# A two-layer hybrid encoder trunk on one core: mixers and norms emitted in fine parts between runs of dense matmuls

## The chip, the cores and the metric

The kernel runs on one core of a Trainium2 chip. The metric is the device time of one execution in microseconds. Three runs of the kernel before took 2494.32, 2494.62 and 2501.36 us; the median is 2494.62 us.

## The reference, cut to what matters

The input x is 1024 tokens of 1024 features, float32. Two layers are applied, each with its own weights:

```python
h = x
for l in range(2):
    mixed = hybrid_mixer(rmsnorm(h, norm_pre_mix[l]), ...)          # w_in -> 3 mixers -> w_out
    h = h + rmsnorm(mixed, norm_post_mix[l])
    ff = squared_relu_mlp(rmsnorm(h, norm_pre_ffn[l]), w_ff1[l], w_ff2[l])   # 1024 -> 4096 -> 1024
    h = h + rmsnorm(ff, norm_post_ffn[l])
return h
```

`hybrid_mixer` projects its normalised input once. From the columns it feeds three causal token mixers: an mLSTM (4 heads of 128 values), a gated linear attention (4 heads of 64) and a retention (4 heads of 64). All carry a state along the sequence. Each head's output is normalised and gated, and the concatenation goes through `w_out`. `rmsnorm` needs the sum of squares of a token over all 1024 features before any feature of it can go on.

## The kernel before, in words

**Tiling.** The sequence is cut into two halves of 512 tokens. A layer and a half make a unit with four dense stages: the input projection (`main`, 8 column groups, then `gates`, 4 groups), the output projection `out_proj` (4 groups), and the MLP `ffn_steps` (8 chunks of 512 hidden features; each chunk has two `f1` groups and four `f2` groups, so 16 and 32 steps). Dense work stands in `fm_group` and `tm_group`. Every float32 product is made of three float32r matmuls (`mm3`, L217 to L220). A group of `fm_group` with 1024 rows holds 48 matmuls of 512 columns, one with 512 rows (`f2`) holds 24; a group of `tm_group` holds 96 matmuls of 256 to 272 columns.

**Weights.** `wslot` (L206) brings 512 rows of a weight: a DMA into `raw`, a copy on ScalarE into `whi`, a subtraction on VectorE into `wlo`. Each of the three has 3 buffers, and all loads are requested 6000 places ahead in the order of the groups.

**Mixers.** `mixer` (L397) does 256 tokens, so each unit has two passes. A pass has gate rows (a transpose `rt`, scans, a second transpose `st`), a convolution, the GLA scores in seven levels (operands `Qg`, `Kg` on VectorE, then the matmuls `gs`), the rotary step, and for each of two chunks of 128 tokens: mLSTM scores `ms`, numerator `mn`, state `mk` and `mu`, retention scores `rs`, outputs `gr`, states `gk` and `gu`, the head norms on ScalarE and VectorE, and transposes `yp` with a product `gt` (L702) that is stored to `pj.y` in DRAM (L703). `load_y` (L718) reads it back, one tile of 128 features for all 512 tokens at a time, and splits it for `out_proj`; so each tile that `out_proj` reads needs the last chunk of the unit.

**Norms.** `post_norm` and `pre_norm` take a sum of squares `ss`, spread it over the partitions with a float32 matmul by ones (`nps_...`, L277), make 1/sqrt on ScalarE and VectorE, and then go through 8 tiles. `mix_norms` runs after `out_proj` (post_mix, sum of squares, pre_ffn), `ffn_norms` after the MLP (post_ffn, sum of squares, the next layer's pre_mix or the output).

**Order.** The kernel is written as one stream of instructions. A scheduler at build time makes each engine's fixed order from it: of the instructions that it takes to be ready, the one with the earliest place in the stream goes first. `tc.high_priority(offset=n)` moves a place n instructions ahead: 6000 for weights, 9000 for emptying PSUM, 2500 for norms. At run time the orders do not change, and an engine whose next instruction is not ready waits.

In the stream, the mixer of layer 0, half 0 stands whole between its unit's `gates` and the next unit's `main` (L997). The three other mixers are spread over the MLP of the other half by `weave` (L825): six parts at the first step, then 1.3 parts a step, of 56 parts. `mix_norms` and `ffn_norms` stand in one piece, 2500 places ahead.

Of the kernel before, what the change touches and what calls it, by code (L numbers as in the profile page):

```python
# [46 lines left out]
def hybrid_trunk(ctx, tc, a, out):  # L47
# [50 lines left out]
    # ---------------------------------------------------------------- parameters  # L98
    # rows of 128 features, transposed on the tensor engine
# [44 lines left out]
    def rotary(hold):  # L144
# [32 lines left out]
        # every later function is in this one set  # L177
# [13 lines left out]
    # block-diagonal operands and states, zero off the blocks  # L191
# [30 lines left out]
    def split(src, name):  # L222
        """float32 [P, 512] as two float32r parts that sum to it."""
# [6 lines left out]
    def fm_group(w, u, evac, name):  # L230
        """w: [1024 or 512, 256] weight columns; out: features on partitions, 2 tiles."""
# [3 lines left out]
        for k in range(nk):  # L235
            for m in range(2):
# [4 lines left out]
                if k == nk - 1:  # L241
                    with tc.high_priority(offset=EPRIO):
                        rest = evac(m, ps[m])
                    if rest:
                        with tc.high_priority(offset=RPRIO):
                            rest()

    def tm_group(w, u, evac, name):
        """w: [1024, n] weight columns; out: tokens on partitions, one tile a chunk."""
        n = w.shape[1]  # L250
        sl = [wslot(w[512 * k:512 * (k + 1), :], n, f"{name}_{k}") for k in range(2)]
        for c in range(NC):
# [15 lines left out]
    def newton(r, v, t):  # L268
        """One step of r <- 1/sqrt(v); v and t are lost."""
# [4 lines left out]
    def rstd_of(ss, name):  # L274
        """1/sqrt(mean over features + eps) on every partition, from the sums of squares."""
        ps = psc.tile([P, 512], F32, tag="sc", name=f"nps_{name}")
        PE.matmul(ps, ones, ss, start=True, stop=True)  # L277
        v = np_.tile([P, TH], F32, tag="nt", name=f"nv_{name}", bufs=3)
# [19 lines left out]
    def pre_norm(h, l, key, name):  # L298
        """h: 8 tiles of the residual; returns the normalised input, split."""
        r = rstd_of(square_sum(h, name), name)  # L300
# [7 lines left out]
    def post_norm(half, acc, ss, l, key, name, store):  # L308
        """acc: 8 tiles of a block's output, turned in place into the new residual."""
        r = rstd_of(ss, name)  # L310
# [9 lines left out]
    # ---------------------------------------------------------------- input projection  # L320
# [12 lines left out]
    def gate_evac(pj, t0, silu):  # L333
        """norm gain * sigmoid (or silu) of a projection, to DRAM."""
# [19 lines left out]
    def in_groups(pj, u):  # L354
        """The column groups of the input projection, as closures."""
# [41 lines left out]
    def mixer(pj, prev, q):  # L397
        """Tokens q*256 ... of a half (q is 0 or 1): all three mixers, to pj.y; yields between its parts."""
# [10 lines left out]
        # gate rows  # L409
# [32 lines left out]
        S.activation(out=st[32:36, :], in_=m[:, 1:], func=AF.Exp, scale=-1.0)  # L442
        ps = ptr.tile([P, 512], F32, tag="tr", name=f"st{nm}")
# [6 lines left out]
        # causal depthwise convolution and silu of the mLSTM's q and k  # L450
# [29 lines left out]
        # GLA: decays and the scores of two chunks  # L480
# [32 lines left out]
        ready = level_operands(0, LEVELS[0])  # L513
        # scores on the diagonal
        qk = m1.tile([P, QT], F32, tag="ge", name=f"qk{nm}", bufs=2)
        V.tensor_tensor(out=qk, in0=gq, in1=gk, op=ALU.mult)
        ps = psc.tile([P, 512], F32, tag="sc", name=f"dd{nm}")
        for c in range(2):
            mm = PE.matmul(ps[:, 4 * c:4 * c + 4], qk[:, c * P:(c + 1) * P], hsel, start=True, stop=True)
            if c == 0:  # L520
                behind(mm, ready)
# [4 lines left out]
        G.tensor_tensor(out=Pg8, in0=ident.unsqueeze(1).to_broadcast([P, 8, P]), in1=dd.unsqueeze(2).to_broadcast([P, 8, P]), op=ALU.mult)  # L526
        for li, s in enumerate(LEVELS):
# [24 lines left out]
        # retention: rotary  # L552
# [13 lines left out]
        for c in range(2):  # L566
# [41 lines left out]
            # state  # L608
# [4 lines left out]
            V.tensor_tensor(out=kw, in0=ps[:, 0:256].rearrange("p (h d) -> p h d", h=4), in1=wk.unsqueeze(2).to_broadcast([P, 4, 64]), op=ALU.mult)  # L613
            for r in range(2):
                ps = ptr.tile([P, 512], F32, tag="tr", name=f"mu{cn}_{r}")
# [7 lines left out]
            # ---- retention scores  # L623
            for h in range(4):
                hs = slice(32 * h, 32 * h + 32)
                S.copy(out=Qr[hs, h, :], in_=rqk[hs, 0, cs])
# [8 lines left out]
            # ---- GLA and retention outputs  # L635
# [5 lines left out]
            for h in range(4):  # L641
# [3 lines left out]
            # ---- GLA and retention states  # L645
# [6 lines left out]
                            in1=gout[:, 0:4].unsqueeze(2).to_broadcast([P, 4, 32]), op=ALU.mult)  # L652
            ps = ptr.tile([P, 512], F32, tag="tr", name=f"gu{cn}")
# [10 lines left out]
            # ---- head norms  # L664
# [79 lines left out]
    def block_sq(ss, src, sq, kt):  # L744
        """ss += src^2; sq: scratch."""
# [341 lines left out]
```

## Time and profile before

| | |
|---|---|
| median of three runs | 2494.62 us (2494.32 to 2501.36) |
| span of the profiled execution | 2496.7 us, from the first to the last instruction |
| what lies around the span | the profiled execution's own time is not listed apart from the three runs; its span is 2.1 us above their median |
| TensorE busy | 2425.6 us |
| VectorE, ScalarE, GpSimd busy | 1554.9, 1064.5, 255.8 us |
| DMA, mean over the span | 129 GB/s |

The busy time of a matmul in the profile overlaps that of the next one, since they are pipelined: a dense matmul of 512 columns is shown with about 400 ns, while the next one starts some 231 ns later. So starts are to be compared, and waits; the busy share alone says little. Names such as `d_f` stand for the PSUM tile of a group (`d_in`, `d_out`, `d_f` for input projection, output projection, MLP), and numbers of buffers are left out of names.

### The profile page before, as it was taken

The page shows a single profiled execution, that of the slowest core. Times are in us where ns is not written, and L with a number is a line of the kernel's source. Part 1 is how long each engine was busy: PE and PEld are TensorE (multiplying, and loading weights), DVE is VectorE, ACT ScalarE, POOL GpSimd, SP SyncE. Part 2 cuts the span into 40 slices and gives each one's busy share as a digit, 9 for nine tenths or more (in the row PEclk, how much of TensorE's full clock was granted, in tenths as well). Part 3 has the DMA queues.
Part 4 walks back from the last instruction along what each step waited for, and adds up shares of the span by engine and source line. Part 5 has one row for each costly group of instructions (what it writes and reads, how often), then busy time and mean ns, then how long its engine had stood idle before and what let it go on. Part 6 is the DMA issues. An engine that isn't in the chain of part 4 may idle for free.

```text
span 2496.7 us, 31320 instructions
## 1 busy us (share of the span) xinstructions
PE 2425.6 (97%) x11436; PEld 1978.3 (79%) x11436; DVE 1554.9 (62%) x2882; ACT 1064.5 (43%) x2035; POOL 255.8 (10%) x249
## 2 busy tenths in 40 slices
PE   7999999999999999999999999999999999999998
PEld 7887787787788788788788778878878877788886
DVE  5659958847655775665855487475685448634344
ACT  5664457334332554633423255563333345332223
POOL 2100000101101110011100111011010101111110
PEclk9999999999999999999999999999999999999999
DMA  7754455334232565433323355633332344433231
GB/s 232 221 144 144 137 173 185 91 110 123 77 107 90 163 205 178 133 99 102 116 87 102 106 178 181 182 121 95 117 109 83 90 134 152 143 93 93 93 99 62
DMA packets 323670, 321.61 MB, mean 129 GB/s; under 512 B 15370, under 2 KB 292412, under 8 KB 323516
## 3 DMA queue, kind: packets, MB, share of 16 engines
q1 hardware_dynamic: 323516, 319.61, 41.6%
q8 instruction: 90, 1.47, 0.3%
q14 instruction: 64, 0.52, 0.1%
HBM read 263.92 MB, written 55.64 MB: 128 GB/s over the span
## 4 chain that ended last, share of the span: by engine, by line
PE 55%; issue 18%; DVE 13%; DMA 3%; POOL 3%; ACT 2%; SPq 0%; POOLq 0%; DVEq 0%; ACTq 0%
PE d_f L218 10%; PE d_f L219 10%; PE d_f L220 10%; PE d_in L219 4%; PE d_in L218 4%; PE d_in L220 4%; POOL r_hid L769 3%; PE d_out L219 2%; PE d_out L218 2%; PE d_out L220 2%; DVE Qg L510 1%; DMA hl_pm<-hD 1%; DVE l_f L214 1%; PE gs L533 1%; DVE Pg L537 1%
## 5 line engine op out<-in xcount | busy, mean ns | idle before, releaser
L213 ACT CAST h_f<-r_f 128x1024 fp32r<-128x1024 f32 x256 | 267.8, 1046 | 662.5 <-PE d_f L220 656.8
L214 DVE TENSOR_TENSOR l_f<-r_f,h_f 128x1024 fp32r<-128x1024 f32 x256 | 321.2, 1255 | 204.2 <-ACT h_f L213 203.3
L218 PE MATMUL d_f<-h_hid,l_f 128*128 128x512 f32 x1024 | 413.4, 404 | 2.1 <-DVE f L789 2.1
L218 PE MATMUL d_f<-uh_uf,l_f 128*128 128x512 f32 x1024 | 409.4, 400 | 1.6 <-ACT uh_uf L226 1.6
L219 PE MATMUL d_f<-l_hid,h_f 128*128 128x512 f32 x1024 | 407.1, 398 | 2.1 <-DVE l_hid L770 2.1
L219 PE MATMUL d_f<-ul_uf,h_f 128*128 128x512 f32 x1024 | 408.2, 399 | 0.6 <-DVE ul_uf L227 0.5
L220 PE MATMUL d_f<-h_hid,h_f 128*128 128x512 f32 x1024 | 405.4, 396 | 0.0
L220 PE MATMUL d_f<-uh_uf,h_f 128*128 128x512 f32 x1024 | 405.1, 396 | 0.0
L769 POOL TENSOR_TENSOR r_hid<-r_hid 128x512 f32<-128x512 f32 x128 | 165.2, 1290 | 1140.7 <-ACT h_hid L768 1112.2
L789 DVE TENSOR_TENSOR f<-f,d_f 128x512 f32<-128x512 f32 x224 | 153.3, 684 | 155.6 <-PE d_f L220 154.4
L218 PEld LDWEIGHTS d_f<-h_hid,l_f 128*128 128x128 f32 x1024 | 193.0, 189 | 49.7 <-DVE f L789 5.0
L218 PEld LDWEIGHTS d_f<-uh_uf,l_f 128*128 128x128 f32 x1024 | 192.7, 188 | 47.6 <-issue 2.3
L219 PEld LDWEIGHTS d_f<-l_hid,h_f 128*128 128x128 f32 x1024 | 192.6, 188 | 44.6 <-DVE l_hid L770 3.4
L220 PEld LDWEIGHTS d_f<-uh_uf,h_f 128*128 128x128 f32 x1024 | 192.4, 188 | 44.7 <-issue 0.9
L219 PEld LDWEIGHTS d_f<-ul_uf,h_f 128*128 128x128 f32 x1024 | 192.5, 188 | 43.9 <-DVE ul_uf L227 1.8
L220 PEld LDWEIGHTS d_f<-h_hid,h_f 128*128 128x128 f32 x1024 | 192.4, 188 | 43.7 <-issue 0.2
L770 DVE TENSOR_TENSOR l_hid<-r_hid,h_hid 128x512 fp32r<-128x512 f32 x128 | 88.3, 690 | 181.7 <-POOL r_hid L769 181.7
L214 DVE TENSOR_TENSOR l_in<-r_in,h_in 128x1024 fp32r<-128x1024 f32 (+2 forms) x96 | 118.8, 1238 | 74.0 <-ACT h_in L213 72.1
L765 ACT ACTIVATE r_hid<-d_f 128x512 f32<-128x512 f32 x128 | 76.5, 598 | 182.4 <-PE d_f L220 182.4
L213 ACT CAST h_in<-r_in 128x1024 fp32r<-128x1024 f32 (+2 forms) x96 | 101.3, 1055 | 43.2 <-PE d_in L220 29.0
L218 PE MATMUL d_in<-uh_x,l_in 128*128 128x512 f32 x256 | 104.7, 409 | 2.3 <-ACT pv L369 1.8
L219 PE MATMUL d_in<-ul_x,h_in 128*128 128x512 f32 x256 | 103.6, 405 | 0.0
(356 smaller groups left out, 4214.5 us busy)
## 6 DMA issues: line engine op xcount, KB each, us to landing
r_f<-in_w_ff_dram SPq DMA_DIRECT2D x256, 512.0 KB, 3.6
r_in<-in_w_in_dram SPq DMA_DIRECT2D x80, 512.0 KB, 3.9
r_out<-in_w_out_dram SPq DMA_DIRECT2D x32, 512.0 KB, 3.5
pv<-pv SPq DMA_DIRECT2D x64, 128.0 KB, 2.7
hl_pm<-hD SPq DMA_DIRECT2D x32, 256.0 KB, 4.4
pf<-px SPq DMA_DIRECT2D x32, 256.0 KB, 4.3
vt<-pv SPq DMA_DIRECT2D x32, 256.0 KB, 3.8
pg<-gz_g SPq DMA_DIRECT2D x32, 256.0 KB, 2.3
```

The costliest lines, as they stand in the source:

```text
L213: S.copy(out=hi[:, :, :n], in_=raw[:, :, :n])
L214: V.tensor_tensor(out=lo[:, :, :n], in0=raw[:, :, :n], in1=hi[:, :, :n].bitcast(F32), op=ALU.subtract)
L218: PE.matmul(ps, al, bh, start=start, stop=False)
L219: PE.matmul(ps, ah, bl, start=False, stop=False)
L220: PE.matmul(ps, ah, bh, start=False, stop=stop)
L510: V.tensor_tensor(out=qb[hs, h, :].rearrange("p (n s) -> p n s", s=s), in0=gqv[hs, :, 1, :], in1=ev[hs, :, 1, :], op=ALU.mult)
L533: mm = PE.matmul(ps[:, c * 256:(c + 1) * 256], kb[:, c * P:(c + 1) * P], qb[:, :, c * 64:(c + 1) * 64], start=True, stop=True)
L537: V.copy_predicated(out=Pg.rearrange("p c h (n w s) -> p (c h) n w s", w=2, s=s)[:, :, :, 1, :], mask=lvm[:, li * 64:(li + 1) * 64].rearra ...
L765: S.activation(out=r, in_=ps, func=AF.Relu)
L769: G.tensor_tensor(out=r, in0=r, in1=r, op=ALU.mult)
L770: V.tensor_tensor(out=lo, in0=r, in1=hi.bitcast(F32), op=ALU.subtract)
L789: V.tensor_tensor(out=t, in0=t, in1=ps, op=ALU.add)
```

## The change

`side`, `tick`, `beside` and `flush` are new. A generator is put beside the dense work with a rate; each call of `tick` adds the rate to its account and advances it by one part for each whole unit. `fm_group` calls `tick` after every 12 matmuls, `tm_group` after every 24 of its half as wide ones. `weave` goes. The mixer has 37 parts in a pass instead of 28: the producers on ScalarE and VectorE of some matmuls stand one part ahead of them. The second `mu` matmul uses another PSUM pool. The two `behind` edges of the diagonal scores go. `mix_norms` and `ffn_norms` become generators: they start after two ticks and let seven ticks pass between the two norms, and the matmul by ones stands at its place in the stream, no longer 2500 places ahead. Removed comments are not shown.

```diff
+    side = []
+    def tick():
+        for g in list(side):
+            g[2] += g[1]
+            while g[2] >= 1 and g in side:
+                g[2] -= 1
+                if next(g[0], 0) == 0:
+                    side.remove(g)
+    def beside(gen, rate=1.0, due=0.0):
+        g = [gen, rate, due]
+        side.append(g)
+        return g
+    def flush(*gs):
+        for g in gs:
+            if g in side:
+                side.remove(g)
+                for _ in g[0]:
+                    pass
...
 # fm_group, for each k and m; tm_group, for each chunk
+                tick()
...
     def rstd_of(ss, name):
+        return rstd_end(rstd_begin(ss, name), ss, name)
+    def rstd_begin(ss, name):
         ps = psc.tile([P, 512], F32, tag="sc", name=f"nps_{name}")
         PE.matmul(ps, ones, ss, start=True, stop=True)
+        return ps
...
 # mixer: new yields after the gate rows' last activation, after qk and the first
 # level's operands, after Pg, after the Qm copies, after kw (with the Qr copies,
 # which stood after the state), and after kt_
             for r in range(2):
-                ps = ptr.tile([P, 512], F32, tag="tr", name=f"mu{cn}_{r}")
+                ps = (psc if r else ptr).tile([P, 512], F32, tag="sc" if r else "tr", name=f"mu{cn}_{r}")
...
-    def weave(parts, steps):
...
-    def mix_norms(l, half, acc, ss):
+    def mix_norms(l, half, acc, ss, res, gap):
+        for _ in range(gap[0]):
+            yield 1
+        n = f"pm{l}{half}"
+        ps = rstd_begin(ss, n)
         with tc.high_priority(offset=NPRIO):
-            h = post_norm(half, acc, ss, l, "post_mix", f"pm{l}{half}", True)
-            return pre_norm(h, l, "pre_ffn", f"uf{l}{half}"), h
+            h = post_norm_end(half, acc, rstd_end(ps, ss, n), l, "post_mix", n, True)
+            n = f"uf{l}{half}"
+            ss = square_sum(h, n)
+        for _ in range(gap[1]):
+            yield 1
+        ps = rstd_begin(ss, n)
+        with tc.high_priority(offset=NPRIO):
+            res["u"] = pre_norm_end(h, rstd_end(ps, ss, n), l, "pre_ffn", n)
+        res["h"] = h
... # ffn_norms in the same way; final yields after each of its 4 chunks
+    AFTER, NEXT = 2, 7
+    MIX = 0.58
-    run(main[2:] + gates)
-    for _ in mix(pj[0, 0], None):
-        pass
+    run(main[2:])
+    m = beside(mix(pj[0, 0], None), 1.35)
+    run(gates)
     pj[0, 1] = Proj(0, 1)
     main, gates = in_groups(pj[0, 1], u[1])
     run(main)
+    flush(m)
     o = out_proj(pj[0, 0], load_y(pj[0, 0]))
-    uf0, _ = mix_norms(0, 0, *o)
+    r = {}
+    g = beside(mix_norms(0, 0, *o, r, (AFTER, NEXT)))
     run(gates)
-    steps, st = ffn_steps(0, 0, uf0)
-    weave(mix(pj[0, 1], pj[0, 0]), steps)
+    flush(g)
+    steps, st = ffn_steps(0, 0, r["u"])
+    m = beside(mix(pj[0, 1], pj[0, 0]), MIX)
+    run(steps)
+    flush(m)
     y = load_y(pj[0, 1])
-    u[0] = ffn_norms(0, 0, st)
+    g = beside(ffn_norms(0, 0, st, r, (AFTER, NEXT)))
     o = out_proj(pj[0, 1], y, mixer_tiles("01"))
-    uf1, _ = mix_norms(0, 1, *o)
+    flush(g)
     pj[1, 0] = Proj(1, 0)
-    main, gates = in_groups(pj[1, 0], u[0])
-    run(main + gates)
-    steps, st = ffn_steps(0, 1, uf1)
-    weave(mix(pj[1, 0], None), steps)
+    main, gates = in_groups(pj[1, 0], r["u"])
+    g = beside(mix_norms(0, 1, *o, r, (AFTER, NEXT)))
+    run(main)
+    flush(g)
+    m = beside(mix(pj[1, 0], None), MIX)
+    run(gates)
+    steps, st = ffn_steps(0, 1, r["u"])
+    run(steps)
+    flush(m)
... # layer 1 likewise; its last mixer is beside gates and steps[:-7]:
+    run(steps[:-7])
+    flush(m)
     o = out_proj(pj[1, 1], load_y(pj[1, 1]), mixer_tiles("11"))
+    g = beside(mix_norms(1, 1, *o, r, (AFTER, NEXT)))
     run(steps[-7:])
+    flush(g)
+    done, finish = last_norm(1, residual_tokens(r["h"]))
+    g = beside(ffn_norms(1, 0, st, r, (AFTER, 2)), 0.5)
     steps, st = ffn_steps(1, 1, r["u"], done=done)
     run(steps)
+    flush(g)
```

## Rows read from the trace of the kernel before

**Rows 1.** The profile's page: busy us of each engine, share of span, instructions.

```profile
PE 2425.6 (97%) x11436; PEld 1978.3 (79%) x11436; DVE 1554.9 (62%) x2882; ACT 1064.5 (43%) x2035; POOL 255.8 (10%) x249
```

**Rows 2.** Waits of TensorE, whole span: waiter, awaited, total us, times, longest.

```profile
PE gs L533 <- DVE Kg L511: 10.0, 11, 1.7
PE nps_uf L277 <- DVE ss_uf L295: 8.2, 4, 2.5
PE nps_u L277 <- DVE ss_u L295: 4.0, 2, 2.2
PE mn L602 <- DVE qi L597: 3.9, 2, 2.1
PE mu L616 <- DVE Cst L620: 3.1, 4, 0.9
...
PE ops L920 <- DVE f L315: 2.4, 4, 0.8
PE d_f L218 <- DVE f L789: 2.1, 4, 0.5
...
PE st L445 <- ACT gi L439: 1.9, 2, 1.3
```

**Rows 3.** Windows by stage: us, then busy of each engine, clock, DMA share, GB/s.

```profile
127.90:172.40 44.50, 43.23 (x180) 34.98 (x181) 18.55 (x22) 30.55 (x47) 0.00 (x0) 0.96 0.52 147
172.40:327.60 155.20, 147.82 (x886) 126.17 (x885) 140.48 (x399) 74.32 (x222) 5.30 (x9) 1.00 0.50 151
...
423.20:846.50 423.30, 412.84 (x1845) 331.06 (x1844) 272.54 (x532) 157.35 (x323) 47.89 (x45) 1.00 0.35 105
846.50:894.80 48.30, 46.45 (x197) 36.64 (x197) 40.83 (x52) 28.51 (x44) 8.97 (x4) 1.00 0.56 176
894.80:1034.60 139.80, 137.88 (x774) 119.51 (x773) 82.75 (x122) 75.98 (x118) 6.67 (x5) 1.00 0.59 181
...
2067.80:2112.00 44.20, 42.28 (x181) 32.79 (x180) 40.17 (x53) 22.56 (x33) 7.14 (x4) 1.00 0.56 179
2112.00:2496.70 384.70, 371.49 (x1645) 298.18 (x1643) 177.52 (x216) 125.22 (x171) 41.90 (x32) 0.99 0.31 96
```

**Rows 4.** Timeline, layer 0 half 0, mixer's last chunk to out_proj: start us, us, engine.

```profile
291.55 1.03 PE L587 MATMUL ms<-Qm,mqk 128*128 128x256 f32 x4
...
315.78 0.68 DVE L702 TENSOR_TENSOR gt<-yp,gt 128x512 f32<-128x512 f32 x1
...
327.65 0.39 PE L218 MATMUL d_out<-uh_y,l_out 128*128 128x512 f32 x1
...
371.89 0.39 PE L220 MATMUL d_out<-uh_y,h_out 128*128 128x512 f32 x1
```

**Rows 5.** Tiles py, ul_y and gt: duration ns min/median/max; DMA landing us (py, ul_y).

```profile
DMA to landing us min/median/max: 2.3/3.8/4.7
...
DMA to landing us min/median/max: 3.2/3.8/4.7
...
L725 ACT CAST uh_y<-ul_y x32: 603/618/626, 321.3 to 2030.7; 128x512 fp32r<-128x512 f32 x32
L702 DVE TENSOR_TENSOR gt<-yp,gt x32: 681/686/692, 225.3 to 2008.4; 128x512 f32<-128x512 f32 x32
```

**Rows 6.** Timeline of SP's queue: weights of out_proj are issued from here.

```profile
820.17 0.37 SPq L210 DMA_DIRECT2D r_out<-in_w_out_dram  x1
```

**Rows 7.** Timeline of TensorE: the two matmuls by ones of mix_norms(0, 0).

```profile
375.83 1.07 PE L277 MATMUL nps_pm<-sso,ones 128*128 128x512 f32 x2
...
409.51 1.88 PE L277 MATMUL nps_uf<-ss_uf,ones 128*128 128x512 f32 x2 [2.38 <-DVE ss_uf L295]
```

**Rows 8.** Timeline of VectorE: last tiles of two pre-norms.

```profile
434.33 1.27 DVE L227 TENSOR_TENSOR ul_uf<-w_uf,uh_uf 128x512 fp32r<-128x512 f32 x2
...
898.02 0.68 DVE L227 TENSOR_TENSOR ul_u<-w_u,uh_u 128x512 fp32r<-128x512 f32 x1
```

**Rows 9.** Window after the wait in rows 7, columns as in rows 3.

```profile
409.50:413.50 4.00, 3.99 (x9) 2.50 (x10) 2.74 (x4) 4.00 (x8) 0.00 (x0) 0.57 0.71 240
```

More of the change, by code (lines that the diff above doesn't have):

```diff
@@ L260, in tm_group @@
                 evac(c, ps)
+            tick()
     def sumsq_add(ss, sq, first, eng=V):
@@ L298, in pre_norm, with pre_norm_end @@
     def pre_norm(h, l, key, name):
-        r = rstd_of(square_sum(h, name), name)
+        ss = square_sum(h, name)
+        return pre_norm_end(h, rstd_of(ss, name), l, key, name)
+    def pre_norm_end(h, r, l, key, name):
         u = []
@@ L308, in post_norm, with post_norm_end @@
     def post_norm(half, acc, ss, l, key, name, store):
-        r = rstd_of(ss, name)
+        return post_norm_end(half, acc, rstd_of(ss, name), l, key, name, store)
+    def post_norm_end(half, acc, r, l, key, name, store):
         for kt in range(KT):
@@ L511, in level_operands @@
             return V.tensor_tensor(out=kb.rearrange("p (n w s) -> p n w s", w=2, s=s)[:, :, 0, :], in0=gkv[:, :, 0, :], in1=ev[:, :, 0, :], op=ALU.mult)
-        ready = level_operands(0, LEVELS[0])
         qk = m1.tile([P, QT], F32, tag="ge", name=f"qk{nm}", bufs=2)
         V.tensor_tensor(out=qk, in0=gq, in1=gk, op=ALU.mult)
+        ready = level_operands(0, LEVELS[0])
+        yield
         ps = psc.tile([P, 512], F32, tag="sc", name=f"dd{nm}")
         for c in range(2):
-            mm = PE.matmul(ps[:, 4 * c:4 * c + 4], qk[:, c * P:(c + 1) * P], hsel, start=True, stop=True)
-            if c == 0:
-                behind(mm, ready)
+            PE.matmul(ps[:, 4 * c:4 * c + 4], qk[:, c * P:(c + 1) * P], hsel, start=True, stop=True)
         dd = m1.tile([P, 8], F32, tag="dd", name=f"dd{nm}")
@@ L613, in mixer @@
             V.tensor_tensor(out=kw, in0=ps[:, 0:256].rearrange("p (h d) -> p h d", h=4), in1=wk.unsqueeze(2).to_broadcast([P, 4, 64]), op=ALU.mult)
+            for h in range(4):
+                hs = slice(32 * h, 32 * h + 32)
+                S.copy(out=Qr[hs, h, :], in_=rqk[hs, 0, cs])
+            yield
             for r in range(2):
-                ps = ptr.tile([P, 512], F32, tag="tr", name=f"mu{cn}_{r}")
+                ps = (psc if r else ptr).tile([P, 512], F32, tag="sc" if r else "tr", name=f"mu{cn}_{r}")
                 PE.matmul(ps[:, 0:258], kw[:, 2 * r:2 * r + 2, :], vt[:, r * 258:(r + 1) * 258], start=True, stop=True)
@@ L622, in mixer @@
             yield
-            for h in range(4):
-                hs = slice(32 * h, 32 * h + 32)
-                S.copy(out=Qr[hs, h, :], in_=rqk[hs, 0, cs])
             psr = psc.tile([P, 512], F32, tag="sc", name=f"rs{cn}")
@@ L823, in mix @@
             yield from mixer(pj, prev, q)
-    def weave(parts, steps):
-        due = 6
-        for s in steps:
-            while due >= 1 and next(parts, 0) is None:
-                due -= 1
-            due = max(due, 0) + 1.3
-            s()
-        for _ in parts:
-            pass
     x_last = []
@@ L899, in hybrid_trunk, with ffn_norms @@
     ffn = {}
-    def mix_norms(l, half, acc, ss):
-        with tc.high_priority(offset=NPRIO):
-            h = post_norm(half, acc, ss, l, "post_mix", f"pm{l}{half}", True)
-            return pre_norm(h, l, "pre_ffn", f"uf{l}{half}"), h
-    def ffn_norms(l, half, st):
-        with tc.high_priority(offset=NPRIO):
-            h = post_norm(half, st["acc"], st["ss"], l, "post_ffn", f"pf{l}{half}", l + 1 < DEPTH)
-            if l + 1 < DEPTH:
-                return pre_norm(h, l + 1, "pre_mix", f"u{l + 1}{half}")
-        final(half, h)
-        return None
+    def mix_norms(l, half, acc, ss, res, gap):
[3 more added lines that the diff above has]
+        ps = rstd_begin(ss, n)
+        with tc.high_priority(offset=NPRIO):
+            h = post_norm_end(half, acc, rstd_end(ps, ss, n), l, "post_mix", n, True)
[4 more added lines that the diff above has]
+        ps = rstd_begin(ss, n)
+        with tc.high_priority(offset=NPRIO):
+            res["u"] = pre_norm_end(h, rstd_end(ps, ss, n), l, "pre_ffn", n)
+        res["h"] = h
+    def ffn_norms(l, half, st, res, gap):
+        for _ in range(gap[0]):
+            yield 1
+        n = f"pf{l}{half}"
+        ps = rstd_begin(st["ss"], n)
+        with tc.high_priority(offset=NPRIO):
+            h = post_norm_end(half, st["acc"], rstd_end(ps, st["ss"], n), l, "post_ffn", n, l + 1 < DEPTH)
+            if l + 1 < DEPTH:
+                n = f"u{l + 1}{half}"
+                ss = square_sum(h, n)
+        for _ in range(gap[1]):
+            yield 1
+        if l + 1 == DEPTH:
+            yield from final(half, h)
+            return
+        ps = rstd_begin(ss, n)
+        with tc.high_priority(offset=NPRIO):
+            res["u"] = pre_norm_end(h, rstd_end(ps, ss, n), l + 1, "pre_mix", n)
     def final(half, h):
@@ L926, in final @@
             dma(out=out[0, r0:r0 + P, :], in_=ot)
+            yield 1
     def residual_tokens(h):
@@ L1001, in hybrid_trunk @@
     run(main)
+    flush(m)
     o = out_proj(pj[0, 0], load_y(pj[0, 0]))
[L1003 removed]
+    r = {}
+    g = beside(mix_norms(0, 0, *o, r, (AFTER, NEXT)))
     run(gates)
[L1005 to L1006 removed]
+    flush(g)
[3 more added lines that the diff above has]
+    flush(m)
     y = load_y(pj[0, 1])
[L1008 removed]
+    g = beside(ffn_norms(0, 0, st, r, (AFTER, NEXT)))
     o = out_proj(pj[0, 1], y, mixer_tiles("01"))
[L1010 removed]
+    flush(g)
     pj[1, 0] = Proj(1, 0)
[L1013 to L1016 removed]
+    main, gates = in_groups(pj[1, 0], r["u"])
[7 more added lines that the diff above has]
+    flush(m)
     y = load_y(pj[1, 0])
[L1018 removed]
+    g = beside(ffn_norms(0, 1, st, r, (AFTER, NEXT)))
     o = out_proj(pj[1, 0], y, mixer_tiles("10"))
[L1020 removed]
+    flush(g)
     pj[1, 1] = Proj(1, 1)
[L1022 to L1025 removed]
+    main, gates = in_groups(pj[1, 1], r["u"])
+    g = beside(mix_norms(1, 0, *o, r, (AFTER, NEXT)))
+    run(main)
+    flush(g)
+    m = beside(mix(pj[1, 1], pj[1, 0]), MIX)
+    run(gates)
+    steps, st = ffn_steps(1, 0, r["u"], late=True)
+    run(steps[:-7])
+    flush(m)
     o = out_proj(pj[1, 1], load_y(pj[1, 1]), mixer_tiles("11"))
+    g = beside(mix_norms(1, 1, *o, r, (AFTER, NEXT)))
     run(steps[-7:])
[L1028 to L1031 removed]
+    flush(g)
+    done, finish = last_norm(1, residual_tokens(r["h"]))
+    g = beside(ffn_norms(1, 0, st, r, (AFTER, 2)), 0.5)
+    steps, st = ffn_steps(1, 1, r["u"], done=done)
     run(steps)
+    flush(g)
     finish(1, st["ss"], st["last"])
```

16 lines of the change are left out of this document (5 added, 11 removed).

## Prediction

> **What bounds the kernel now.** I read the page's busy times first, then the waits of TensorE, then a table of windows cut at the stage borders, and last the timeline around each border. TensorE is shown busy for 97% of the span [rows 1], so the end is set by its one fixed order of matmuls. That share hides small losses, so starts are compared: `out_proj` of layer 0, half 0 has 192 matmuls, the first at 327.65 and the last at 371.89, which makes 44.24 / 191 = 0.232 us a matmul [rows 4]. An MLP has 1536 of them, 356 us, yet the first one takes 423.3 us [rows 3]; the other 67 us are a mixer's own matmuls and waits. The table of waits names what ends last: VectorE, in the seven GLA levels (`gs`, 10.0 us in all), in the two sums of squares before a norm (`nps`, 8.2 + 4.0), and in the mLSTM (`mn` 3.9, `mu` 3.1) [rows 2]. So at most some 35 us of named waits can be won, and what the change makes TensorE wait for anew is set against that.
>
> **What stays.** No arithmetic goes or comes but two small moves; the same matmuls, DMAs and splits are issued. A switch between mixer and dense matmuls is not an item: mixer blocks are about as many as before (most parts hold one), and the second `mu` in another bank joins two of them. So the sum is one of waits. Six terms follow.
>
> **A. First mixer, 127.9 to 327.65.** Before, it began behind the gates, and the whole of it was due before the next `main`. Now it is beside the gates (16 ticks) and `main` (32 ticks) at 1.35, which issues 64 of 74 parts; the last ten come at once in front of `out_proj`, which needs them. Dense work: gates 44.5 us; `main` about 90 (the stretch of the next unit's `main` and gates takes 139.8 [rows 3], less 44.5, less some 5 for two matmuls by ones and their wait). A mixer's matmuls: 67 us in the first MLP less about 10 of waits, so 57 with its small losses; that fits here too (155.2 = 90 + 57 + 8). The ten parts hold 58 of a mixer's 308 matmul records, 19%. So dense work ends at 127.9 + 44.5 + 90 + 46 + 3 of waits left = 311.5. Then TensorE has only the tail: scores, numerator, outputs, head norms, `yp`, the store of y, its load, its split. Before, from the last chunk's `ms` to `out_proj` took 36.1 us [rows 4], with VectorE busy for 140.5 of 155.2 us [rows 3] and dense work between: the upper end. If half of the 24 us up to `gt` was that crowding, and y's way is 9 us (see C), it is 21: the lower end. I take 24, nearer to the low end since nothing else is due then: `out_proj` starts at 335.5, **+8 us** (from -3, with the small losses gone as well, to +20). Gates of the next unit do not fill the hole: weights are brought in the order of the groups into three buffers, and `out_proj`'s are under way 26 us ahead of it at 820.17 [rows 6], so they occupy the buffers that gates would need.
>
> **B. Norms start later.** The matmul by ones loses its 2500 places. Before, `nps_pm` ran 16 matmuls behind `out_proj`'s end (375.83 against 372.1) [rows 4, 7]; now its place is behind three ticks, 36 matmuls: 20 x 0.232 = 4.6 us later, and so is all behind it. The second one does not gain from its seven ticks: from the first to the second took 33.7 us [rows 7], seven ticks are 84 x 0.232 = 19.5 us, so it is late at its place and runs as soon as it is thought ready, as before; I leave its waits in. Where dense work needs the result at once the delay shows. The MLP of unit (0, 0) began at 423.2 while VectorE made its last input at 435.6; `main` of unit (1, 0) began at 894.8 and its last input came at 898.7 [rows 3, 8]: no slack. Three places are of this kind (MLP of (0, 0), `main` of (1, 1), MLP of (1, 1); at `main` of (1, 0) the hole of C covers it): 3.5 + 2.5 + 3 = **+9** (0, if VectorE catches up, to 14, three times 4.6).
>
> **C. End of the first MLP, 846.5.** 128 ticks x 0.58 = 74.24: the 74th part, the last `yp`, comes in the very last tick. Then y must be multiplied (0.69), stored (median landing 3.8), loaded (3.8) and copied (0.62) [rows 5] with nothing else for TensorE: 8.9 us; the next three tiles come slower than they are used, about 1; and the lower clock behind a pause costs 1.7 (behind a wait of 2.38 us the granted clock was 0.57 over 4 us, so 1.2 of 2.4 GHz for most of it and 43% of 4 us lost [rows 7, 9]). 11.5, less the `nps_u` wait of 2.2 [rows 2], which gets slack from the hole: **+9** (from 0.7 + 2.3 + 3.2 + 0.6 - 2.2 = 4.6, to 0.7 + 4.7 + 4.7 + 0.6 + 1.7 + 3 - 2.2 = 13, if y's splits queue on VectorE behind the norm, which is 2500 places ahead). What is queued behind: `out_proj` and all dense work.
>
> Of the clock the Trainium skill (TensorE: Matmul & The Clock Gate, section "HAM oscillation — how this bites in real kernels") says that waits for DMA between batches of matmuls bring TensorE back to its low clock, and that short pauses do not; by it A and D would pay the clock too and the sum would be 3 us more. The row differs in one point, since a pause of 2.38 us was enough here.
>
> The Trainium skill (DMA: Bandwidth & Descriptors, section "Latency and other measured facts") puts the fixed cost of a DMA at about 2 us and says that it shrinks with a lightly loaded memory; by it a store and a load alone in the queue would save, as an estimate, 2 to 3 us of the 7.6, and C would be +6. The landings here run from 2.3 to 4.7, so the median is kept.
>
> **D. Last mixer.** It is beside gates (16 ticks) and 114 ticks of MLP, and ends at tick 128 of 130: 24 matmuls, 5.6 us, lie between `yp` and `out_proj`, against some 10 for y: **+4.5** (1 to 8). The mixer of unit (1, 0) ends 16 ticks ahead: nothing.
>
> **E. Three mixers beside MLPs.** Parts come 20.7 matmuls (4.8 us) apart, evenly, with producers a part ahead. Of `gs` 10.0, `mu` 3.1 and `d_f` behind `f` 2.1 [rows 2] most goes; `st` stays, since its chain is longer than a part: **-13.5** (-6, if VectorE cannot hold the rate in the levels; -19, if `st` and small losses go too).
>
> **F. End.** The transposes of the output wait 2.4 us [rows 2]; they get room, but the last MLP's first accumulators need the tiles that they read: **-1** (-3 to +2).
>
> **Sum.** 8 + 9 + 9 + 4.5 - 13.5 - 1 = +16 us on a span of 2496.7, so 2512.7. The span stands 2.1 us above the median of the runs, so I predict **2510.5 us**.
>
> **The rivals.**
>
> *VectorE is what was late (faster).* One mechanism: with even parts VectorE has no backlog. For it: in A's stretch it is busy 91% [rows 3], and nearly all waits name it [rows 2]. Then the tail of A is short (-3), B is caught up (0), C and D take their low ends (+4.6, +1), E its full -19, F -1: -17, 2478; it decides if B is under 3 and E beyond -16. Against it: store and load of y (7.6 us at the median) are no work of VectorE. Half way there is 2483.
>
> *Gains and losses cancel.* C at +7, D +3, A 0, B +2, E -11, F -1: 0, 2494.6. That also stands for the change not doing what it says, where the scheduler's estimate of readiness and not the place sets the order: then E is about -4, and A, B, C small for the same reason. For it: `gs` waits are spread over 11 times, most under 1 us [rows 2].
>
> *The tail is as long as before (much slower).* At 1.35 parts a tick VectorE falls behind in the levels; the tail of A is 36 us (+20), C at its upper end (+13), B 12, E -7: +41 with D, 2536. Against it: VectorE's work, 18.6 + 140.5 us, now has from 127.9 on instead of from 172.4 [rows 3].
>
> **How the numbers follow.** Forecast (2500 to 2522) 0.44; faster rival 0.26; cancelling 0.18; much slower 0.12. The bounds of all terms give -19 to +51; two in ten left out, the range is 2481 to 2537; the forecast's own is 2502 to 2520. A measurement of this kernel tells about 0.3% (7.5 us) from no change: faster 0.26, within 0.3% 0.20 (the cancelling case and the forecast's low edge), slower 0.54.
>
> **What would show it.** A: a hole in TensorE ahead of the first `d_out`, ended by the copy `uh_y`, and that start at 330 to 345. B: `nps_pm` and `nps_pf` 36 matmuls behind the stage border; waits for `ul_uf` or `ul_u`. C, D: the same hole of 9 to 13 us and of about 5. E: `gs` waits below 4 us in all. The prediction is wrong if `out_proj` follows without a hole at these borders, or if the stretch of an MLP shrinks by more than 8 us.

## The result, and the profile after

The changed kernel takes 2527.75 us (median of 4 runs, 2525.58 to 2530.11) beside 2495.3 us for the kernel before: ratio of the runs 1.0117 [1.0096, 1.0139], which is 29 us slower (the medians alone lie 32.5 apart). The forecast was 2510.5 us, slower; the side and the places were right, the size was half. The profiled execution took 2527.24 us with a span of 2525.4, 28.7 more than before. Its busy line:

```profile
PE 2429.1 (96%) x11436; PEld 1990.0 (79%) x11436; DVE 1543.9 (61%) x2882; ACT 1063.7 (42%) x2035; POOL 255.3 (10%) x249
```

The instructions are the same in number and TensorE is busy for 3.5 us more than in [rows 1], so the loss is time in which it waits or runs at its low clock. Summed over all rows of the view, its waits take 86.7 us, 60.7 before. The rows on which the readings below rest (waiter, awaited, total us, times, longest):

```profile
PE d_out L242 <- ACT uh_y L766: 12.8, 3, 4.6
PE nps_uf L306 <- DVE ss_uf L327: 7.3, 4, 2.7
PE yp L742 <- DVE gt L743: 7.1, 9, 1.0
PE yp L742 <- DVE y L732: 6.0, 1, 6.0
PE dd L558 <- ACT ge L429: 4.8, 1, 4.8
PE d_out L243 <- DVE ul_y L767: 4.7, 1, 4.7
PE gs L571 <- DVE Kg L549: 3.8, 6, 1.5
...
PE nps_u L306 <- DVE ss_u L327: 3.2, 1, 3.2
...
PE d_f L243 <- DVE ul_uf L251: 1.7, 1, 1.7
```

Beside [rows 2], `gs` fell from 10.0 to 3.8 and `mu` is gone from the list. In their place stand waits that the kernel before does not have (`dd` had 0.3 there): y's copies `uh_y` and `ul_y`, 17.5 us, the tail of the first mixer (`y`, 6.0), `dd`, and the transposes `yp` of one PSUM bank that wait for each other's reader `gt`. By stages (us; busy of PE, PEld, DVE, ACT, POOL; clock; DMA share; GB/s):

```profile
174.00:315.00 141.00, 138.99 (x835) 121.37 (x834) 101.07 (x267) 63.88 (x175) 2.88 (x6) 1.00 0.51 152
315.00:339.20 24.20, 11.81 (x64) 8.76 (x62) 21.85 (x62) 9.74 (x35) 0.10 (x1) 0.74 0.53 163
339.20:386.00 46.80, 46.80 (x193) 37.38 (x194) 22.96 (x34) 22.99 (x37) 0.09 (x1) 0.95 0.42 130
386.00:444.00 58.00, 49.80 (x212) 38.99 (x210) 42.09 (x60) 43.86 (x71) 7.25 (x6) 0.96 0.61 195
444.00:857.40 413.40, 409.27 (x1819) 332.00 (x1820) 254.45 (x501) 143.97 (x297) 47.56 (x43) 0.99 0.32 97
...
866.70:919.30 52.60, 47.92 (x194) 37.69 (x195) 38.81 (x55) 29.54 (x47) 6.24 (x4) 0.91 0.55 175
```

The borders are the first dense matmul of each stage. Set against those of before they give the ledger of the 28.7 us:

| stretch | before | after | difference |
|---|---|---|---|
| to `out_proj` (0,0) | 327.65 | 339.15 | +11.5 |
| `out_proj` (0,0) | 44.5 | 46.8 | +2.4 |
| gates and norms, to the MLP of (0,0) | 51.2 | 58.0 | +6.8 |
| MLP (0,0) | 423.2 | 413.5 | -9.7 |
| hole ahead of `out_proj` (0,1) | 0 | 9.2 | +9.2 |
| `out_proj` (0,1) | 48.3 | 52.6 | +4.3 |
| `main` and gates (1,0) | 139.9 | 146.5 | +6.6 |
| MLP (0,1) | 417.4 | 408.0 | -9.4 |
| `out_proj` (1,0) | 50.3 | 49.6 | -0.7 |
| `main` and gates (1,1) | 142.0 | 150.1 | +8.1 |
| MLP (1,0), to `out_proj` (1,1), a hole of 3.6 in it | 376.9 | 372.1 | -4.8 |
| all that follows | 475.3 | 479.8 | +4.5 |

The three MLPs with a mixer win 27.5 us together (9.7, 9.4, and 4.8 with the hole of 3.6 taken out); the rest loses 56.3. Part of the win is mixer work that only moved, out of the MLPs into the gates and into the holes.

### The profile page after: what moved, and what is told of

Same layout as the page of the kernel before. It is cut to its first block, busy times and chain, and to the rows that moved or that the text cites. A ratio compares the mean times of both kernels' runs of the same rounds, so it can differ in the third digit from the quotient of the medians.

```text
span 2525.4 us, 31270 instructions
## 1 busy us (share of the span) xinstructions
PE 2429.1 (96%) x11436; PEld 1990.0 (79%) x11436; DVE 1543.9 (61%) x2882; ACT 1063.7 (42%) x2035; POOL 255.3 (10%) x249
## 4 chain that ended last, share of the span: by engine, by line
PE 59%; issue 20%; DVE 10%; DMA 4%; POOL 3%; ACT 3%; SPq 0%; POOLq 0%; DVEq 0%; ACTq 0%
PE d_f L243 11%; PE d_f L242 11%; PE d_f L244 11%; PE d_in L242 4%; PE d_in L243 4%; PE d_in L244 4%; POOL r_hid L810 3%; PE d_out L243 2%; PE d_out L242 2%; PE d_out L244 2%; PE gs L571 2%; DMA hl_pm<-hD 1%; DVE l_in L238 1%; DVE l_f L238 1%; PE mn L644 1%
## 5 line engine op out<-in xcount | busy, mean ns | idle before, releaser
L242 PE MATMUL d_f<-uh_uf,l_f 128*128 128x512 f32 x1024 | 418.0, 409 | 1.6 <-ACT uh_uf L250 1.6
L242 PEld LDWEIGHTS d_f<-uh_uf,l_f 128*128 128x128 f32 x1024 | 193.8, 189 | 49.5 <-issue 3.9
L243 PEld LDWEIGHTS d_f<-ul_uf,h_f 128*128 128x128 f32 x1024 | 193.2, 189 | 46.8 <-issue 3.1
L237 ACT CAST h_in<-r_in 128x1024 fp32r<-128x1024 f32 (+2 forms) x96 | 101.1, 1054 | 49.6 <-PE d_in L244 27.9
L242 PE MATMUL d_out<-uh_y,l_out 128*128 128x512 f32 x256 | 104.1, 409 | 12.8 <-ACT uh_y L766 12.8
```

Source lines behind the costliest of these rows:

```text
L237: S.copy(out=hi[:, :, :n], in_=raw[:, :, :n])
L242: PE.matmul(ps, al, bh, start=start, stop=False)
L243: PE.matmul(ps, ah, bl, start=False, stop=False)
```

## What stands at the borders

*First mixer.* TensorE ahead of `out_proj` (0,0) (start us, us, engine, operation, in brackets the wait), then two rows of VectorE from that hole:

```profile
314.98 0.28 PE L244 MATMUL d_in<-h_in,uh_x 128*128 128x256 f32 x1
...
329.96 1.09 PE L742 MATMUL yp<-c_a,y 128*128 128x128 f32 x4 [6.01 <-DVE y L732]
...
339.15 1.22 PE L242 MATMUL d_out<-uh_y,l_out 128*128 128x512 f32 x2 [4.57 <-ACT uh_y L766]
```

```profile
326.04 0.48 DVE L506 SCALAR_TENSOR_TENSOR mqk<-cv,prm,mqk 128x256 f32<-128x256 f32 x1
...
329.40 0.74 DVE L732 TENSOR_TENSOR y<-mn,scl 128x256 f32<-128x256 f32 x2
```

From the last dense matmul to `out_proj` pass 24.2 us; with nothing dense between, VectorE puts the convolution of the next mixer (L504, L506) between the steps of this one's head norms: six of these instructions, some 2.4 us, between 326.0 and the `y` of 329.4.

*End of the first MLP.* TensorE, then VectorE, in the same stretch:

```profile
859.19 0.66 PE L742 MATMUL yp<-c_a,y 128*128 128x128 f32 x4 [0.95 <-DVE gt L743]
...
866.65 1.22 PE L242 MATMUL d_out<-uh_y,l_out 128*128 128x512 f32 x2 [4.61 <-ACT uh_y L766]
872.56 0.80 PE L243 MATMUL d_out<-ul_y,h_out 128*128 128x512 f32 x1 [4.68 <-DVE ul_y L767]
```

```profile
868.21 3.70 DVE L351 TENSOR_TENSOR f<-f,ssf 128x512 f32<-128x512 f32 x6
871.82 0.68 DVE L767 TENSOR_TENSOR ul_y<-ul_y,uh_y 128x512 fp32r<-128x512 f32 x1
```

There are two waits. The first is y's way through DRAM. The second is a queue: six tiles of the post-norm, 3.7 us, run on VectorE ahead of the first split of y, for which TensorE stands.

*Norms.* The matmuls by ones of `mix_norms` (0,0), and what TensorE has behind them:

```profile
394.33 1.02 PE L306 MATMUL nps_pm<-sso,ones 128*128 128x512 f32 x2
...
433.26 1.13 PE L306 MATMUL nps_uf<-ss_uf,ones 128*128 128x512 f32 x2 [1.77 <-DVE ss_uf L327]
...
441.35 0.99 PE L558 MATMUL dd<-c_a,qk 128*128 128x4 f32 x4 [4.81 <-ACT ge L429]
443.96 0.79 PE L242 MATMUL d_f<-uh_uf,l_f 128*128 128x512 f32 x1 [1.62 <-ACT uh_uf L250]
```

The last wait ahead of the MLP is for the norm's own `uh_uf`, so the norm sets the start; the wait for `dd` lies in front of it. The border costs more than its stretch shows: in windows of 2 us the granted clock is 0.58 from 439 and 0.50 from 441 to 453. From 443.96 to 453.0 only 16 dense matmuls are done, which take 3.7 us at 0.232, and one of them waits 1.7 for `ul_uf`. So some 5.3 us are lost inside the stretch that the ledger gives to the MLP of (0,0).

## The experiments

Each ratio is to the kernel before, run beside it on the same chip, with its 95% interval. Between runs the chip can differ, so a difference of two ratios carries both intervals: 5 to 7 us for the differences below. The kernels are the changed one unless the text says otherwise. My theory was that of the prediction: the finer parts win, and what was late at the borders (A, B, C, D) costs more. The main rivals were that the finer interleaving itself costs, and that an edit at a border only moves the wait.

**a_first**, the first mixer done before `main` ends:

```diff
-    m = beside(mix(pj[0, 0], None), 1.35)
+    m = beside(mix(pj[0, 0], None), 1.6)
     run(gates)
+    m[1] = 2.0
```

> The changed kernel with one edit: the first mixer runs at 1.6 parts a tick beside the gates and at 2.0 beside main, so its last part comes about 8 ticks (22 us) ahead of out_proj. Theory of the exposed tails: the hole of 24 us ahead of the first out_proj goes, the tail's 6 us of mixer matmuls move in front of it, and the low clock behind the hole goes too: -14 to -18 us against the changed kernel, so about 2511. Rival (fine interleaving itself costs, by VectorE falling behind): the waits before gs grow at the higher rate and eat most of it, -5 us or less.

Measured: 1.0059 [1.0042, 1.0076], 14.5 us (0.0058 of 2497) under the changed kernel. `out_proj` follows at once:

```profile
330.17 0.28 PE L244 MATMUL d_in<-h_in,uh_x 128*128 128x256 f32 x1
330.29 0.39 PE L242 MATMUL d_out<-uh_y,l_out 128*128 128x512 f32 x1
```

So the mixer fits beside gates and `main` in 330 us, against 339 with a tail; the tail was a matter of rate, not of room.

**c_mlp**, the first MLP's mixer at 0.66 instead of 0.58 a tick:

> The changed kernel with one edit: the mixer beside the first MLP runs at 0.66 instead of 0.58 parts a tick and ends 15 ticks (42 us) ahead of out_proj. Theory of the exposed tails: the hole of 9.2 us and the waits for y inside out_proj (4.3 us) go, and of the norm's lateness 2 to 4 us come back at the next input projection: -9 to -13 us, about 2517. Rival (fine interleaving itself costs): within 3 us of the changed kernel.

Measured: 1.0076 [1.0057, 1.0096], 10 us less. The hole is gone, and with it the cover of the norm's wait, which stood at 1.9 before and 0 in the changed kernel at this border:

```profile
860.66 0.39 PE L244 MATMUL d_f<-h_hid,h_f 128*128 128x512 f32 x1
860.89 0.40 PE L242 MATMUL d_out<-uh_y,l_out 128*128 128x512 f32 x1
...
899.65 2.07 PE L306 MATMUL nps_u<-ss_u,ones 128*128 128x512 f32 x2 [3.21 <-DVE ss_u L327]
```

**b_nps**, the matmuls by ones with their 2500 places again, the gaps between norms kept:

```diff
-        ps = rstd_begin(ss, n)
         with tc.high_priority(offset=NPRIO):
+            ps = rstd_begin(ss, n)
```

> The changed kernel with the matmuls by ones back at 2500 places ahead, the gaps of 2 and 7 ticks kept. Theory of the late norms: all behind the first one starts 20 matmuls (4.6 us) sooner where dense work waits for it, at the MLP of (0,0), main of (1,1) and the MLP of (1,1): -5 to -12 us, about 2519. Rival (the order follows readiness, the place of the matmul by ones does not matter; the norms are late because VectorE and the loads of the residual are slower in the new mix): within 3 us.

Measured: 1.0071 [1.0053, 1.0089], 11.5 us less. The MLP starts 49.5 us behind the end of `out_proj` (385.2) instead of 58.0; both matmuls come sooner, the time between them is 33.75 us again, and the wait for `dd` is not there. The granted clock is 1.00 throughout from 432 to 444, so the loss inside the MLP's start is gone too:

```profile
388.87 1.06 PE L306 MATMUL nps_pm<-sso,ones 128*128 128x512 f32 x2
...
422.62 1.13 PE L306 MATMUL nps_uf<-ss_uf,ones 128*128 128x512 f32 x2 [2.45 <-DVE ss_uf L327]
434.70 0.40 PE L242 MATMUL d_f<-uh_uf,l_f 128*128 128x512 f32 x1
```

**d_last**, the last mixer at 0.66:

> The changed kernel with one number changed: the last mixer, that of unit (1,1), is advanced at 0.66 instead of 0.58 a tick, so it ends some 14 ticks ahead of out_proj (1,1). If term D is what its hole shows (3.6 us of TensorE waiting for uh_y at 2041.6), the hole goes and the kernel is 2.5 to 5 us faster than the changed one: ratio to before 1.0095 to 1.0110. Rival (out_proj follows at once, and the norm behind it is late by as much): 1.0112 to 1.0125.

Measured: 1.0098 [1.0083, 1.0114]. The hole of 3.6 us ahead of `out_proj` (1,1) is gone (the stretch from the MLP's start falls from 372.1 to 367.3), but the last stretch is 2.6 longer in this profile. The 4.7 us between the two ratios are less than their intervals: the place is shown, the gain is not.

**abcd**, those four edits together:

> All three edits together, and 0.66 for the last mixer as well (its hole of 4 us). Theory of tails and late norms: the terms add up to -35 to -44 us, about 2488, which is 7 us under the kernel before. Rival (fine interleaving itself costs): stays above 2505.

Measured: 0.9977 [0.9965, 0.9988]: 35 us under the changed kernel (14.5 + 10 + 11.5 + 4.7 = 41 by the single edits, whose differences have intervals of about 7 us each), and 6 under the one before. Four edits of place and rate, with the finer parts kept, turn the change's sign, so the finer parts are not what costs. It came at the weak end of what I expected of it (35 to 44 under the changed kernel); `nps_uf` still waits 10.5 us in four places, 4.3 at the longest.

**b_tail**, C alone put into the kernel before: the weave at 1.05 instead of 1.3 in the first MLP.

> The kernel before, with one number changed: the mixer that is spread over the first MLP is advanced at 1.05 instead of 1.3 parts per 12 matmuls, so that its last parts come in the last ticks of that MLP; norms, first mixer and parts are those of before. My theory (what costs is y left for TensorE to wait for at the end of an MLP, whoever spreads the mixer): a hole of 9 to 13 us before the first d_out of out_proj (0,1) and slow y tiles behind it, 10 to 14 us slower than before, ratio 1.004 to 1.0056. Rival (in the changed kernel it is the finer, later mixer, or its norms, that costs there, and the place of its end does not matter): ratio 0.999 to 1.001.

Measured: 1.0068 [1.0054, 1.0081], 17 us slower, more than either side expected of it. The same two waits stand in its trace:

```profile
854.74 1.22 PE L218 MATMUL d_out<-uh_y,l_out 128*128 128x512 f32 x2 [5.24 <-ACT uh_y L725]
860.02 0.80 PE L219 MATMUL d_out<-ul_y,h_out 128*128 128x512 f32 x1 [4.06 <-DVE ul_y L726]
```

Behind them the clock is low (windows as above, from the end of the MLP on):

```profile
844.90:854.70 9.80, 2.55 (x12) 1.18 (x10) 7.27 (x11) 4.11 (x6) 0.00 (x0) 0.77 0.69 212
854.70:858.70 4.00, 1.22 (x2) 0.50 (x2) 4.00 (x8) 3.83 (x7) 1.03 (x1) 0.50 1.00 355
858.70:862.70 4.00, 2.08 (x4) 1.16 (x4) 4.00 (x6) 1.02 (x2) 2.64 (x2) 0.50 0.56 204
862.70:866.70 4.00, 3.67 (x7) 2.03 (x8) 4.00 (x4) 1.16 (x3) 2.95 (x2) 0.50 0.70 243
```

In 12 us from `out_proj`'s start only 13 matmuls are done, where 52 (12 / 0.232) are done otherwise; VectorE is busy in all of it. Where a mixer ends is thus dear by itself, with the old parts and the old norms too.

**e_fine**, E alone: the three mixers beside MLPs in the finer parts at 0.66, 0.58 and 0.66 a tick (the last two from the gates on), the first mixer whole behind the gates, the norms in one piece, as before.

> Term E by itself: only the three mixers beside the MLPs are in the finer parts and advanced by the ticks (0.66, 0.58 and 0.66 a tick, so that each ends ahead of its MLP); the first mixer is issued whole behind the gates and the norms are in one piece with their 2500 places, as before. My theory (the finer parts win 13 to 16 us, and the changed kernel lost more at its ends): 11 to 16 us faster than before, ratio 0.9936 to 0.9956. Rival (the finer parts win by half at most, and the rest of the gain in abcd came from the first mixer): ratio 0.997 to 1.000.

Measured: 0.9968 [0.9955, 0.9982], 8 us faster: between the theory and the rival, nearer the rival. In its profile the stages that hold the mixers (MLP (0,0); `main` to `out_proj` of the two others) sum to 1483.9 us against 1499.5 before, 15.6 less; 3.0 of it is lost before 330.7 us, where the work is the same but for the cut of the first mixer, and 3.1 in the other stages, so that the last dense matmul starts 9.5 earlier. TensorE's waits sum to 55.5 us, 60.7 before.

To see which half of E wins, the parts and the schedule (the even rate, and for two mixers the start beside the gates) were taken apart. **e_coarse**: e_fine with the mixer body of before (56 parts, both `mu` in one bank), at 0.5, 0.44 and 0.5 a tick.

> e_fine with the mixer cut into the 56 parts of before (and both state products mu in one bank), advanced by the ticks at 0.5, 0.44 and 0.5, so that each mixer keeps its place. e_fine was 0.9968 of before. If the finer cut is what wins, this is as before: 0.9985 to 1.0015. Rival (the even rate and the earlier start win): 0.996 to 0.998, as e_fine.

Measured: 0.9996 [0.9986, 1.0006]. **e_weave**: the kernel before with the finer parts, spread over the steps as before:

```diff
-        due = 6
+        due = 8
...
-            due = max(due, 0) + 1.3
+            due = max(due, 0) + 1.72
```

> The kernel before with the 74 finer parts, spread as before over the steps of an MLP (1.72 parts a step instead of 1.3, 8 ahead instead of 6; a step is 24 or 48 matmuls). If the finer cut is what wins: 0.996 to 0.998. Rival (the even rate wins): 0.999 to 1.0015.

Measured: 1.0008 [0.9999, 1.0017]. Neither half wins alone: e_coarse speaks against the schedule as what wins, e_weave against the cut. TensorE's waits sum to 60.6 us in e_coarse and 66.9 in e_weave. Some of them, e_coarse, then e_weave, then e_fine:

```profile
PE st L482 <- DVE st L478: 7.0, 5, 2.4
...
PE gs L570 <- DVE Kg L548: 3.0, 4, 1.7
```

```profile
PE gs L534 <- DVE Kg L512: 7.8, 7, 2.6
```

```profile
PE gs L571 <- DVE Kg L549: 1.2, 1, 1.2
...
PE st L483 <- DVE st L478: 1.8, 2, 1.5
```

Set beside the 10.0 of [rows 2]: the even rate alone takes `gs` down but leaves `st` waiting in the same part as its producer; the finer cut alone leaves bursts of parts between steps of 48 matmuls, where `gs` still waits 7.8. My reading is that only the cut and the schedule together give each part its producer one part earlier and the time between. For `gs` the rows show it. For `st` they do not: with all that it waits for, it has 7.3 in e_coarse, 5.4 in e_weave and 4.8 in e_fine, but 3.3 before. And `nps_uf` waits 9.9 and 12.0 in the two halves against 8.0 in e_fine, which the cut does not explain. The even rate and the earlier start were not tried apart.

**e_gap**, e_fine with 16 ticks between the two sums over features beside `main`, in two units, the second at its own place:

```diff
-    now(mix_norms(0, 1, *o, r, (AFTER, NEXT)))
+    g = beside(mix_norms(0, 1, *o, r, (0, 16)))
     run(main)
+    flush(g)
```

> As e_fine, and the norms between out_proj and MLP of units (0,1) and (1,0) are advanced beside main, with 16 ticks between the first sum over features and the second; the second matmul by ones is issued behind those 16 ticks at its own place. 16 x 12 x 0.232 = 44 us is longer than the 33 to 38 us from the first to the second, so the wait of TensorE for the second (nps_uf, 2 to 4 us at either place) should go: 3 to 7 us faster than e_fine, ratio to before 0.991 to 0.994. Rival (the gap only moves the wait, to the inputs u of the MLP behind it): the same as e_fine within 0.1%.

Measured: 0.994 [0.9926, 0.9954], 7 us under e_fine. The matmul by ones of (0,1), in e_fine, then in e_gap:

```profile
934.17 1.13 PE L306 MATMUL nps_uf<-ss_uf,ones 128*128 128x512 f32 x2 [2.43 <-DVE ss_uf L327]
```

```profile
939.96 1.02 PE L306 MATMUL nps_uf<-ss_uf,ones 128*128 128x512 f32 x2
```

A gap longer than the chain between the two sums ends the wait here. So a set place for a norm is good where the gap covers the chain; the change's seven ticks (19.5 us) do not.

**abcd_gap**, abcd with those gaps, and 6 ticks at full rate in the norm beside the last MLP:

> As abcd, with 16 ticks instead of 7 between the two sums over features beside main, the second at its own place, and the norm beside the last MLP at twice the rate with 6 ticks between. If nps_uf (4.5 and 3.3 us beside main in abcd) and the transposes of the output (ops, 4.3 us) waited only for their place, 6 to 12 us faster than abcd: ratio to before 0.993 to 0.9955. Rival (the waits are of VectorE's load and only move): within 0.1% of abcd, 0.997 to 0.9985.

Measured: 0.9925 [0.9911, 0.9939], 13 us under abcd, a little more than expected.

**best**, abcd_gap with one part more ahead of `st` and the second `yp` of a chunk in the other pool (rates scaled for 76 parts):

```diff
+        yield
...
-                ps = ptr.tile([P, 512], F32, tag="tr", name=f"yp{cn}{g}")
+                ps = (psc if g else ptr).tile([P, 512], F32, tag="sc" if g else "tr", name=f"yp{cn}{g}")
```

> abcd_gap with two edits in the mixer: one part more between the gate rows and the transposes st, and the second yp of a chunk in a bank of the other pool (rates scaled for 76 parts). In abcd_gap TensorE waits 6.1 us for st and gi, 4.3 us for gt (yp and mk). If both go: 6 to 10 us faster than abcd_gap, ratio to before 0.9885 to 0.990. Rival (VectorE and ScalarE are late by their load, so that the waits move to the next parts): 0.992 to 0.993.

Measured: 0.9911 [0.9898, 0.9925], 2477.25 us: the lowest ratio here, 51 us under the changed kernel and 22 under the one before, but only 3.5 under abcd_gap where 6 to 10 were expected, and that is less than the two intervals: a gain over abcd_gap is not shown. `yp` behind `gt` is gone; in the first mixer, where VectorE is fullest ([rows 3]), the wait moved to the levels (waits of abcd_gap, then of best):

```profile
PE gs L571 <- DVE wk L632: 3.9, 2, 2.0
PE yp L742 <- DVE gt L743: 3.4, 4, 0.9
```

```profile
PE gs L572 <- DVE Kg L550: 6.0, 6, 1.9
```

## Why the prediction was right or wrong

The sign and the mechanisms hold: holes at three borders, norms that start later, a gain in each MLP. The size failed: 2527.75 us lies above the forecast's own 2502 to 2520, though inside the wide range. The terms show where; the column "by a run" is the difference of two ratios times 2497 us.

| term | forecast | in the trace | by a run |
|---|---|---|---|
| A, first mixer's tail | +8 | +13.9 | 14.5 (a_first) |
| B, norms later | +9 | +13.9, and 5.3 hidden in E | 11.5 (b_nps) |
| C, end of first MLP | +9 | +13.5 | 10 (c_mlp), 17 into before (b_tail) |
| D, last mixer | +4.5 | +3.6 | 4.7, unclear (d_last) |
| E, three mixers | -13.5 | -19.9 | -8 (e_fine) |
| F, end | -1 | +4.5, B's part in it | not run alone |
| sum | +16 | +28.8, with -0.7 in `out_proj` (1,0) | |

**A.** The tail was right in size, 24.2 us against 24, and in part by luck: the 24 was taken near the low end since nothing else is due then, while VectorE did have the next mixer's convolution to do, and TensorE waited 6.0 for `y` behind it. Two things beside the tail were not right. Dense work ended at 315.0 instead of 311.5, since TensorE still waited 6.0 us behind 129.5 (`gs` 3.8, `st` 1.9, `yp` 0.3) where I had left 3. And I priced nothing behind the hole: `out_proj` ran at the low clock and took 2.4 more. The start of 339.15 was inside the 330 to 345 that I had named.

**B.** `nps_pm` came 36 matmuls behind the border, as forecast. The step that failed is "from the first to the second took 33.7 us" [rows 7]: in the changed kernel it took 38.9. So the MLP of (0,0) started 6.8 later, not 3.5: the first matmul by ones 4.6 later behind the border, the second 5.2 more, and from it to the MLP 10.7 instead of 13.8. The 5.3 lost at the low clock behind the border had no term. For the two `main` stages the trace gives 146.5 and 150.1; e_fine, which also has mixer work in these gates, has 144.6 and 144.9, so 1.9 and 5.2 are the norms' (the other 4.7 and 2.9 are counted in E). With the 2500 places back (b_nps) the chain is 33.75 again, so the place is what made it longer; by which steps I have not separated.

**C.** The first wait was priced well: 9.2 us of hole, by 8.9. What failed is "the next three tiles come slower than they are used, about 1": what was late was the split of the first tile, by 4.7 us, because it queued on VectorE behind six tiles of the norm. That is the case that the prediction put only at its upper end of 13. The forecast that `nps_u` gets slack held: it waits at one border instead of two, and at both again in c_mlp. The 2.2 that I took off for it belongs to the other border; here it had waited 1.9.

The Trainium skill's rule on the clock (TensorE: Matmul & The Clock Gate, "HAM oscillation — how this bites in real kernels"), that waits for DMA between batches bring the low clock, is borne out in D, where I had not priced it: behind the wait of 3.61 us for the copy of a loaded tile the granted clock is 0.68 over 4 us. In A the clock is low behind the hole too (0.50 over 4 us), but it was at 0.50 from 327 us on, in the wait of 6.0 us for VectorE's `y`, before any wait for a DMA. The estimate of 3 us more in the sum was on the right side. The estimate of C at +6 by the Trainium skill (DMA: Bandwidth & Descriptors, "Latency and other measured facts") was not: y's loads landed in 4.5 us at the median, 3.8 before.

**D** came as its hole said. **E** won more in the trace than forecast, because some of the second mixer had slipped forward into the holes of A and B: the MLP of (0,0) is 9.7 shorter than before, even with 5.3 lost at its start, and only 4.5 shorter in e_fine. Of the waits that were to go, `mu` went and `gs` fell to 3.8, but `d_f` behind `f` stayed (2.2), and the 7.1 of `yp` behind `gt` I had not foreseen. Its -19.9 is the three MLPs (-9.7, -9.4, and -4.8 less D's hole of 3.6) with the 4.7 and 2.9 that moved into the gates. Alone it is worth 15.6 us in its own stages and 8 by the clock of the whole kernel; what takes the rest back is open. **F**: the transposes `ops` and the accumulators wait as before; the sign was wrong.

Of the rivals, the much slower one is nearest in time (2536), with the wrong reason: A's tail was not 36 us. VectorE being what was late fell as a reason for a faster kernel: where it is late, the even rate alone does not help (e_coarse), and y's way is not its work but for the split.

Of the signs that I had named, the holes, their ends and the start of `out_proj` came, `nps_pm` came at its place, and `gs` is below 4 us. `nps_pf` did not come 36 matmuls behind the border: it ran in C's hole, at 860.92, before any dense matmul. And one of the signs of being wrong came: the stretch of an MLP shrinks by more than 8 us, in all three cases. Without the 4.7 and 2.9 that only moved into the gates the last two shrink by 4.7 and 5.5; the finer parts do not win 8 us in an MLP, and the sign did not allow for work that moves.

## What to carry over

When work is spread over other work by a rate, look first at where it ends: the last part should come as many matmuls ahead of its reader as its way (store, load, copies) takes, and what is queued on the copying engines ahead of it counts as way. A wait between two dependent steps goes when the gap is longer than their chain (e_gap); moving the second one's place alone (b_nps) won time but left its wait, 2.45 us. A finer cut paid here only together with the even schedule. Price each hole with what follows it, the low clock and the queue: 4.3 us behind the hole of 9.2 at the first MLP's end, 2.4 behind the first mixer's.

## What the runs showed of the hardware

Behind waits that ended at 339.15, 866.65 and 2045.60 (4.6, 4.6 and 3.6 us) the granted clock was 0.50 to 0.68 over the next 4 us, where 0.50 is 1.2 of 2.4 GHz, and where a second wait of 4.7 us followed it was 0.50 over the 4 us after that too. In the first case it had fallen earlier: in windows of 2 us it is 0.92 from 325 and 0.50 from 327 to 343, and TensorE's matmuls between the waits ran at it (windows of the changed kernel from the first `d_out` of A, C and D on):

```profile
339.20:343.20 4.00, 4.00 (x9) 2.68 (x10) 3.58 (x7) 3.12 (x5) 0.00 (x0) 0.50 0.92 316
...
866.70:870.70 4.00, 1.17 (x2) 0.45 (x2) 4.00 (x8) 3.35 (x6) 0.00 (x0) 0.50 1.02 347
870.70:874.70 4.00, 2.14 (x5) 1.38 (x6) 4.00 (x7) 1.25 (x4) 0.00 (x0) 0.50 0.79 292
...
2045.60:2049.60 4.00, 4.00 (x11) 2.89 (x12) 3.33 (x5) 2.49 (x4) 0.00 (x0) 0.68 1.04 349
```

In the first of these windows 9 matmuls are done where 17 are at full clock. The first 4 us of each have a DMA share of 0.92 to 1.04 at 316 to 349 GB/s; in the second of these rows the norm's stores of the residual and loads `hl_pf` are issued between y's loads. Y's loads land later than before (minimum, median, maximum; 3.2/3.8/4.7 in [rows 5]):

```profile
DMA to landing us min/median/max: 3.8/4.5/5.5
```
